# Larger row groups, one-bank column sums with prefix scans, last rows loaded in shrinking pieces, and stores moved to the sync engine, for the diagonal of a 2-D prefix sum

## The chip, the cores and the metric

The kernel runs on one core of a Trainium2 chip. The metric is device time in microseconds (us), the median of several runs. The profile shows one run. Its span, from the first to the last instruction, is 1.6 to 2.2 us shorter than the measured time of these kernels, because it leaves out what lies around the instructions. All times on the time axis below are counted from the start of the span.

Names: PE is the matrix engine, DVE the vector engine, ACT the scalar engine, POOL the GpSimd engine, and SP the sync engine, which computes nothing and here only issues DMAs. In these traces each engine works through its own queue of instructions in order (experiment 8 shows a matmul held up for that reason). A DMA "lands" when the last of the DMA engines that share it, 16 for every load here, has reported its part. PSUM is the memory into which PE adds up its results. A scan is one instruction that writes a running sum along a row.

## The reference

```python
def setup_inputs():
    B, H, W = 4, 4224, 4224
    return {"x": np.random.randn(B, H, W).astype(np.float32)}

def reference(x):
    ps = np.cumsum(np.cumsum(x, axis=1), axis=2)
    diag = np.diagonal(ps, axis1=1, axis2=2)
    return np.cumsum(diag, axis=1).astype(np.float32)
```

The diagonal element `ps[n, n]` is the sum of the square `x[0:n+1, 0:n+1]`. So it grows from n-1 to n by an "L": row n up to the diagonal, and column n above the diagonal. Call that increment `s[n]`. The output is the prefix sum of the prefix sum of `s`. The kernel therefore reads every element once (285 MB), adds the part of each row left of the diagonal along the row (DVE and ACT), adds the part of each column above the diagonal down the column (PE, with a vector of ones), and then does two prefix sums over 4224 numbers per batch.

## The kernel before

It goes through the rows in groups of 256 (two neighbouring rows to a partition), with one group of 128 rows at the end of each batch. POOL loads a group with one DMA that also turns fp32 into bf16. Nine buffers let the loads run far ahead. Row sums go to DVE (`reduce_sum`) and ACT (`activation` with an accumulated sum), column sums to PE, spread over three PSUM tiles.

```python
    groups = [(g * 256, 2) for g in range(16)] + [(4096, 1)]      # shortened
    strips = ctx.enter_context(tc.tile_pool(name="strips", bufs=9))
    ...
        for gi, (row0, pack) in enumerate(groups):
            ...
                strip = strips.tile([P, PACK, N], BF16, name="strip")
                nc.gpsimd.dma_start(out=strip, in_=x[b, row0 : row0 + gw, :].rearrange(...))
            ws = scalar_cols(row0)
            nc.vector.reduce_sum(out=rsv[:, gi, :pack], in_=strip[:, :pack, ws:diag_hi], axis=AX.X)
            for q in range(pack):
                ...                                   # mask the diagonal block, column sums of it on PE
                    nc.scalar.activation(out=dump[:, :ws], in_=strip[:, q, :ws], func=ACT.Copy,
                                         accum_out=sas[:, gi, q : q + 1])
            ...                                       # column sums right of the diagonal on PE
            ...                                       # every 512 columns: copy sums out, scans by single adds
        ...                                           # six fp32 matmuls with triangular weights
        nc.scalar.copy(out=out_sb[nm1 : nm1 + 1, :], in_=out_ps[nm1:NB, :])

        nc.gpsimd.dma_start(
            out=out[b].rearrange("(nb t) -> nb t", t=P), in_=out_sb[:NB, :]
        )
```

POOL issues the loads, and POOL also stores the result.

## Time and profile before

| | |
|---|---|
| time, median of 3 runs | 683.05 us (683.02 to 683.14) |
| span of the profiled run | 681.2 us |
| first load packet | 2.7 us |
| a 256-row group lands every | 9.99 us (4.325 MB read: 433 GB/s) |
| a 128-row group | 5.035 us |
| last load landed | 666.4 us |
| last landing to end of span | 14.8 us |

The rows on packets and landings come from the trace's records of the packets and of the semaphore increments that report them.

First, the page of the kernel before: shares of the span, then the 40 slices of DMA share (9 is 90% or more) and of GB/s written, then the DMA queues with packets, MB and the share of the 16 engines' time.

```profile
PE 181.6 (27%) x1212; PEld 61.6 (9%) x1212; DVE 275.7 (40%) x765; ACT 169.5 (25%) x281; POOL 41.3 (6%) x87
...
DMA  8999999999999999999999999999999999999990
GB/s 179 219 218 210 222 215 213 221 215 214 220 211 221 219 209 222 216 213 221 213 217 220 209 221 220 210 220 217 212 223 214 215 222 210 218 219 213 219 201 3
...
q0 software_dynamic: 9920, 142.81, 98.5%
q8 instruction: 9, 0.15, 0.1%
q14 instruction: 10, 0.08, 0.0%
```

The load queue keeps the DMA engines busy 98.5% of the time and no compute engine is busy for half of it. The GB/s row counts bytes written, which are half of the bytes read, since fp32 becomes bf16: 217 there is 433 read. It is level between the first slice (179) and the last two (201 and 3). The waits say the same. The columns of the next fence are: engine, line, what it waited for, total us, number of waits, longest wait.

```profile
DVE rsv L211 <- DMA strip<-in_x_dram: 337.3, 64, 9.1
...
ACT dump L237 <- DMA strip<-in_x_dram: 290.3, 52, 8.6
...
PE cps L248 <- DMA strip<-in_x_dram: 273.7, 48, 14.2
```

So DVE, ACT and PE wait for data, and work taken from them in the middle of the run gains nothing. What can be gained lies before the first packet, in the rate and the number of bytes and packets, and after the last landing. Here are the two ends of the timeline (start, duration in us, engine, line, operation, and in brackets the idle time before it and what ended it), and the last piece of the chain of work.

```profile
1.31 1.23 POOL L65 DMA_DIRECT2D strip<-in_x_dram  x2 [0.80 <-POOLq L331]
...
14.11 0.69 DVE L211 TENSOR_REDUCE rsv<-strip 128x2 f32<-128x512 bf16 x1 [7.71 <-DMA strip<-in_x_dram]
```

```profile
666.48 2.28 DVE L211 TENSOR_REDUCE rsv<-strip 128x1 f32<-128x2048 bf16 x1
...
673.42 0.26 ACT L312 COPY out_sb<-out_ps 1x128 f32<-1x128 f32 x1 [1.53 <-PE out_ps L309]
673.97 0.53 POOL L314 DMA_DIRECT2D out_dram<-out_sb  x1 [81.42 <-ACT out_sb L312]
```

```profile
673.95 0.55 POOLq L342
```

The last row sum begins at 666.48, when the last group has landed, and the last copy of the result ends at 673.68: 7.2 us of dependent work. Then POOL issues the store. It lands at 675.6, but the span ends at 681.2. The chain's last line names POOL. Behind POOL's last instruction stands a drain, which the page does not count as busy; in the trace it lasts from 673.95 to 680.45, 6.5 us. After it come 0.7 us of a barrier of all engines.

### The profile page before, as it was taken

The page shows a single profiled execution, that of the slowest core. Times are in us where ns is not written, and L with a number is a line of the kernel's source. Part 1 is how long each engine was busy: PE and PEld are TensorE (multiplying, and loading weights), DVE is VectorE, ACT ScalarE, POOL GpSimd, SP SyncE. Part 2 cuts the span into 40 slices and gives each one's busy share as a digit, 9 for nine tenths or more (in the row PEclk, how much of TensorE's full clock was granted, in tenths as well). Part 3 has the DMA queues.
Part 4 walks back from the last instruction along what each step waited for, and adds up shares of the span by engine and source line. Part 5 has one row for each costly group of instructions (what it writes and reads, how often), then busy time and mean ns, then how long its engine had stood idle before and what let it go on. Part 6 is the DMA issues. An engine that isn't in the chain of part 4 may idle for free.

```text
span 681.2 us, 3798 instructions
## 1 busy us (share of the span) xinstructions
PE 181.6 (27%) x1212; PEld 61.6 (9%) x1212; DVE 275.7 (40%) x765; ACT 169.5 (25%) x281; POOL 41.3 (6%) x87
## 2 busy tenths in 40 slices
PE   1243132111442232221233422321124422322112
PEld 0011000000110000000111100000011110000001
DVE  3243245456333333355622342443552323434553
ACT  0001123334101122244400121332440011323442
POOL 2200000000200000000020000000011000000000
PEclk9965555555555555555567555555555555555555
DMA  8999999999999999999999999999999999999990
GB/s 179 219 218 210 222 215 213 221 215 214 220 211 221 219 209 222 216 213 221 213 217 220 209 221 220 210 220 217 212 223 214 215 222 210 218 219 213 219 201 3
DMA packets 9939, 143.04 MB, mean 210 GB/s; under 512 B 1172, under 2 KB 1216, under 8 KB 1216
## 3 DMA queue, kind: packets, MB, share of 16 engines
q0 software_dynamic: 9920, 142.81, 98.5%
q8 instruction: 9, 0.15, 0.1%
q14 instruction: 10, 0.08, 0.0%
HBM read 285.47 MB, written 0.07 MB: 419 GB/s over the span
## 4 chain that ended last, share of the span: by engine, by line
issue 36%; DMA 30%; another core or an unknown queue 21%; DVE 9%; POOL 1%; PE 1%; ACT 1%; POOLq 0%
DMA strip<-in_x_dram 30%; DVE rsv L211 7%; DVE mu L218 1%; POOL strip L203 1%; PE cps L227 1%; ACT c_row L161 1%; DVE cs_col L179 0%; DVE ccs_col L184 0%; PE cps L248 0%; POOL out_dram L314 0%; PE colps L163 0%; DVE aint L261 0%; ACT s_col L283 0%; DVE aint L258 0%
## 5 line engine op out<-in xcount | busy, mean ns | idle before, releaser
L211 DVE TENSOR_REDUCE rsv<-strip 128x2 f32<-128x1536 bf16 (+13 forms) x68 | 178.9, 2630 | 337.3 <-DMA strip<-in_x_dram 337.3
L237 ACT ACTIVATE dump<-strip 128x512 bf16<-128x512 bf16 (+12 forms) x100 | 131.6, 1316 | 291.9 <-DMA strip<-in_x_dram 290.3
L248 PE MATMUL cps<-strip,ones_col 128*1 128x512 bf16 (+2 forms) x640 | 125.7, 530 | 273.7 <-DMA strip<-in_x_dram 273.7
L227 PE MATMUL cps<-mu,ones_col 128*1 128x256 bf16 x132 | 46.8, 372 | 196.0 <-DVE mu L218 196.0
L161 ACT CAST c_row<-cps 1x512 bf16<-1x512 f32 (+1 forms) x36 | 19.4, 540 | 176.0 <-PE cps L248 165.1
L248 PEld LDWEIGHTS <-ones_col 128*1 128x1 bf16 x640 | 27.2, 93 | 304.1 <-issue 300.1
L203 POOL DMA_DIRECT2D strip<-in_x_dram x62 | 32.9, 541 | 297.8 <-DMA strip<-in_x_dram 278.5
L218 DVE SCALAR_TENSOR_TENSOR mu<-strip,um 128x256 bf16<-128x256 bf16 x132 | 49.9, 414 | 0.0
L179 DVE TENSOR_TENSOR cs_col<-cs_col,s_col 128x1 f32<-128x1 f32 x128 | 20.3, 158 | 48.4 <-ACT s_col L283 47.0
L227 PEld LDWEIGHTS <-ones_col 128*1 128x1 bf16 x132 | 13.1, 100 | 229.1 <-issue 228.6
L184 DVE TENSOR_TENSOR ccs_col<-ccs_col,cs_col 128x1 f32<-128x1 f32 x128 | 19.7, 154 | 1.3 <-DVE cs_col L179 0.4
L267 PE MATMUL colps<-aint,sc 128*128 128x1 bf16 x260 | 17.5, 170 | 7.8 <-DVE aint L261 7.8
L314 POOL DMA_DIRECT2D out_dram<-out_sb x4 | 2.1, 534 | 275.2 <-ACT out_sb L312 143.4
L237 ACT ACTIVATION_READ_ACCUMULATOR dump<-strip 128x1 f32 x100 | 18.6, 186 | 0.0
L267 PEld LDWEIGHTS <-sc 128*128 128x128 bf16 x260 | 12.3, 105 | 48.8 <-issue 48.1
L163 PE MATMUL colps<-one_one,c_row 1*128 1x1 bf16 x132 | 9.1, 166 | 12.3 <-ACT c_row L161 11.9
L261 DVE TENSOR_TENSOR aint<-aint,ruv 128x2 bf16<-128x2 bf16 (+1 forms) x68 | 10.9, 160 | 2.1
L218 DVE DVE_READ_ACCUMULATOR mu<-strip,um 128x1 f32 x132 | 10.9, 82 | 0.0
L258 DVE TENSOR_TENSOR aint<-rsv,sas 128x2 bf16<-128x2 f32 (+1 forms) x68 | 10.6, 156 | 0.1
L283 ACT COPY s_col<-colps 128x4 f32<-128x4 f32 (+1 forms) x36 | 5.8, 162 | 14.7 <-PE colps L163 14.7
L147 DVE MEMSET cps<- 128x512 f32 x12 | 5.8, 485 | 4.8 <-ACT c_row L161 4.3
L163 PEld LDWEIGHTS <-c_row 1*128 1x128 bf16 x132 | 6.1, 102 | 14.8 <-ACT c_row L161 14.5
(37 smaller groups left out, 33.9 us busy)
## 6 DMA issues: line engine op xcount, KB each, us to landing
strip<-in_x_dram POOLq DMA_DIRECT2D x64, 2112.0 KB, 74.5
strip<-in_x_dram POOLq DMA_DIRECT2D x4, 1056.0 KB, 74.4
out_dram<-out_sb POOLq DMA_DIRECT2D x4, 16.5 KB, 8.4
```

The source lines that it names most:

```text
L161: nc.scalar.copy(out=c_row[:, lo:hi], in_=chunk_slice(lo, hi))
L163: nc.tensor.matmul(colps[:, k : k + 1], lhsT=c_row[:, k * P : (k + 1) * P], rhs=one_one, start=False, stop=False, skip_group_check=True,)
L179: nc.vector.tensor_add(out=cs_col[:, k + 1 : k + 2], in0=cs_col[:, k : k + 1], in1=s_col[:, k : k + 1],)
L184: nc.vector.tensor_add(out=ccs_col[:, k + 1 : k + 2], in0=ccs_col[:, k : k + 1], in1=cs_col[:, k : k + 1],)
L203: nc.gpsimd.dma_start(out=strip, in_=src)
L211: nc.vector.reduce_sum(out=rsv[:, gi, :pack], in_=strip[:, :pack, ws:diag_hi], axis=AX.X,)
L218: nc.vector.scalar_tensor_tensor(out=mu[:, :gw], in0=strip[:, q, diag_lo:diag_hi], scalar=1.0, in1=upper_masks[pack][q], op0=ALU.mult, op1 ...
L227: nc.tensor.matmul(chunk_slice(diag_lo, diag_hi), lhsT=ones_col, rhs=mu[:, :gw], start=False, stop=False, skip_group_check=True,)
L237: nc.scalar.activation(out=dump[:, :ws], in_=strip[:, q, :ws], func=ACT.Copy, accum_out=sas[:, gi, q : q + 1],)
L248: nc.tensor.matmul(chunk_slice(col, nxt), lhsT=ones_col, rhs=strip[:, q, col:nxt], start=False, stop=False, skip_group_check=True,)
L261: nc.vector.tensor_sub(out=aint[:, gi, :pack], in0=aint[:, gi, :pack], in1=ruv[:, gi, :pack])
L267: nc.tensor.matmul(colps[:, k : k + 1], lhsT=scatters[pack][q][par], rhs=aint[:, gi, q : q + 1], start=False, stop=False, skip_group_check ...
```

## The change

Its intent was to take less time before the first packet and after the last one: groups of 384 rows (three neighbouring rows to a partition, one DMA each); column sums of all groups in one PSUM bank, put into their row of it by a one-hot weight matrix; two scan instructions in place of chains of single adds; the last 384 rows of the last batch loaded in shrinking pieces; the first piece of them (a "head" of 128 rows x 1056 columns) loaded as fp32 by SP at the very start, before POOL's queue gets going; output stores issued by SP. The core of the diff, long parts cut:

```diff
-    PACK = 2
-    GROUP_ROWS = P * PACK
+    F = 3
+    GW = P * F
+    NG = N // GW
-    strips = ctx.enter_context(tc.tile_pool(name="strips", bufs=9))
+    strips = ctx.enter_context(tc.tile_pool(name="strips", bufs=6))
+    HEAD = 1056
+    TB = N - P
+    head = last.tile([P, HEAD], FP32, name="head")
+    nc.sync.dma_start(out=head, in_=x[LB, TB:N, N - HEAD : N])
+    sel = consts.tile([P, 2 * NG - 1], BF16, name="sel")          # zeros, one column of ones
+    def selector(j):
+        return sel[:, NG - 1 - j : 2 * NG - 1 - j]
 ...
+            if j < ng:
+                matmul(d[:, lo:hi], selector(j), rhs, start=first["d"])
 ...
+    def scans(d, rows, width, init1, init2, c12):
+        nc.vector.tensor_tensor_scan(out=c12[:rows, 0, :width], data0=ones_row[:rows, :width],
+            data1=d, initial=init1, op0=ALU.mult, op1=ALU.add)
+        nc.vector.tensor_tensor_scan(...)                         # the same over the first scan
 ...
+        # last batch, rows 3840 to 4095: pieces of columns, the diagonal's first
+        cuts = [r0, 2176, 832, 0]
+        nc.gpsimd.dma_start(out=strip[:, :2, r0:N], in_=src[:, :, r0:N])
+        for c1, c0 in zip(cuts[:-1], cuts[1:]):
+            nc.gpsimd.dma_start(out=strip[:, :2, c0:c1], in_=src[:, :, c0:c1])
+        # the last 128 rows, without the head
+        tcuts = [N - HEAD, 1584, 528, 0]
+        for c1, c0 in zip(tcuts[:-1], tcuts[1:]):
+            nc.gpsimd.dma_start(out=tail[:, 0, c0:c1], in_=x[b, TB:N, c0:c1])
 ...
+        for i, (c1, c0) in enumerate(zip(cuts[:-1], cuts[1:])):
+            ws = (c1 - c0) // 2
+            for q in range(2):
+                act_sum(lsa[:, q, i : i + 1], strip[:, q, c0 : c0 + ws])
+            nc.vector.reduce_sum(out=lrs[:, :, i + 1], in_=strip[:, :2, c0 + ws : c1], axis=AX.X)
+        ...                                                       # lrows = row sums of these 256 rows
+        for q in range(2):
+            matmul(d_last[:, q : gw : 2], lrows[:, q : q + 1], ident)
+        scans(d_last, 1, GW, lcarry[:, 0:1], lcarry[:, 1:2], lc)
+        nc.sync.dma_start(out=out[b, r0 : r0 + gw].unsqueeze(0), in_=lc[:, 1, :gw])
+        ...                                                       # tail: sums tsum, matmuls into fin
+        nc.vector.tensor_add(out=yl, in0=fin, in1=lc[:, 1, gw:GW])
+        nc.sync.dma_start(out=out[b, TB:N].unsqueeze(0), in_=yl)
-        nc.gpsimd.dma_start(
-            out=out[b].rearrange("(nb t) -> nb t", t=P), in_=out_sb[:NB, :]
-        )
```

## The prediction

> **What bounds the kernel now.** The load stream. The page shows the DMA engines 98.5% busy, while DVE is at 40%, PE 27%, ACT 25%; 285.47 MB are read in a 681.2 us span. In the landings of the loads (decoded from the trace), a 256-row strip (4.325 MB read) lands every 9.98 us, 433 GB/s, from start to end, and the 128-row strips take 5.02 us; no gap at the batch borders. The waits agree: DVE, ACT and PE wait mostly for strip DMAs (337, 290, 274 us). So arithmetic in the middle is free.
>
> The span as a sum: first packet at 2.7 us; about 1.4 us of ramp and completion; 64 x 9.98 + 4 x 5.02 = 658.8 us of stream; one DMA engine ends about 3.3 us behind the first (a lag that grows in jumps near instruction-fetch packets); last landing about 666.4. Then (timeline of the end): 7.0 us of arithmetic to the last copy at 673.7; POOL store issued at 674.0, landed about 675.7; POOL's drain, which begins right behind its store, ends only at 680.5, and 0.7 us of barrier follow to 681.2. Tail: 14.7 us.
>
> **What the change does.**
> 1. 384-row groups: longer packets (3 rows instead of 2). From 9.98 against 2 x 5.02 a packet costs some 7.5 ns beyond its bytes, so 43 groups take 642.4 us instead of 643.7. Worth about 1.3 us. The pieces at the end give back about 0.6 us.
> 2. Head (0.54 MB, 1.25 us of stream) on SP at the start: starts perhaps 0.5 us before POOL's loads do. Worth up to 0.5 us.
> 3. Fewer instructions (an estimate from the loops: about 2400 against 3798), so fewer fetches, less lag: 0.5 to 1 us.
> 4. One-hot sums, one bank, scans: hidden chains replace hidden chains. DVE needs about 8.5 us for the widest group (1.04 ns per column), below the 14.9 us it takes to land. Worth 0.
> 5. The tail. The last piece is 528 columns, but DVE runs in order: the strip's reduction (1.0 us), four small sums (0.7), two fp32 matmuls (1.0), two scans (1.2 to 1.9), then the tail's reductions of 792, 1056 and 528 columns (2.9) that queue behind the scans, matmul 0.65, add 0.2. From the last landing that is about 4.5 us instead of 7.0.
> 6. Store on SP: landing about 2 us (estimate; the Trainium skill, "DMA: Bandwidth & Descriptors", section "Anatomy of one DMA", gives about 2.0 us fixed per DMA; the POOL store here took 1.7). The gain is elsewhere: POOL's last instruction becomes a load issued long before, so its 6.5 us drain is hidden, and the end is store + about 0.9 us. Worth nearly 5 us, the largest term.
>
> Tail 4.5 + 2.0 + 0.9 = 7.4 instead of 14.7. Last landing 664.3. Span about 671.7; the measured time is 1.9 us above the span: 673.6 us, 1.4% faster.
>
> **What would show it.** Right: stream at 433 to 435 GB/s; last landing near 664; last landing to end 6.5 to 8.5 us; DVE gapless over the tail reductions behind the scans. Wrong on step 6: POOL's drain still ends last. Wrong on step 1: groups land off 14.94 us.
>
> **What would make it wrong.** Small pieces costing far more per packet; head traffic slowing the first group; scans of 2 us each; or a shorter tail from reordered DVE work plus a larger gain from long packets (then over 2%, below 669.4).
>
> Range 670.3 to 677.0 us. Faster by over 2%: 0.08; within 2%: 0.91; slower: 0.01.

## The result, and the profile after

The kernel after takes 674.39 us (median of 4 runs, 674.34 to 674.50), against 683.03 us for the kernel before in the same rounds. The ratio is 0.9873, with a 95% interval from 0.9859 to 0.9887: 1.3% faster. Here and below a ratio is the mean time of one kernel's fast runs over that of the other's of the same rounds, so it is not quite the ratio of the medians that are quoted.

The page after, the same lines:

```profile
PE 232.5 (35%) x852; PEld 91.2 (14%) x852; DVE 259.3 (39%) x370; ACT 153.9 (23%) x249; POOL 31.8 (5%) x67
...
DMA  9999999999999999999999999999999999999994
GB/s 202 217 215 218 217 217 217 217 217 217 217 219 217 217 218 217 217 217 217 217 217 218 218 217 217 217 215 217 218 217 217 217 217 218 217 217 217 217 201 76
...
q0 software_dynamic: 7712, 142.47, 99.0%
q1 hardware_dynamic: 234, 0.61, 0.3%
q8 instruction: 6, 0.10, 0.1%
q14 instruction: 6, 0.05, 0.0%
```

There are 2608 instructions instead of 3798 and 12 instruction packets instead of 19. SP's queue (q1) appears. The stream is as full and as level as before. DVE's wait is again for the data; PE now waits for DVE's masked block, which waits for the data:

```profile
DVE mu L240 <- DMA strip<-in_x_dram: 380.9, 41, 11.7
PE d L156 <- DVE mu L240: 318.5, 43, 37.2
```

The start and the end of the timeline:

```profile
0.81 0.40 SPq L55 DMA_DIRECT2D head<-in_x_dram  x1
...
1.32 1.19 POOL L60 DMA_DIRECT2D strip<-in_x_dram  x2 [0.80 <-POOLq L384]
...
19.81 1.35 DVE L252 TENSOR_REDUCE rs<-strip 128x3 f32<-128x1152 bf16 x1 [13.92 <-DMA strip<-in_x_dram]
```

SP issues the head at 0.81 and its first packet starts at 1.8; the first packets of POOL's loads follow at 3.5. At the end DVE is the engine to read:

```profile
650.74 6.15 DVE L252 TENSOR_REDUCE rs<-strip 128x3 f32<-128x5760 bf16 x1
...
658.29 1.88 DVE L334 TENSOR_REDUCE lrs<-strip 128x2 f32<-128x1664 bf16 x1
...
663.25 0.98 DVE L334 TENSOR_REDUCE lrs<-strip 128x2 f32<-128x832 bf16 x1
...
665.40 0.96 DVE L362 TENSOR_REDUCE tsum<-strip 128x1 f32<-128x792 bf16 x1
...
666.29 0.14 DVE L343 TENSOR_TENSOR lrows<-l,l 128x2 f32<-128x2 f32 x1
666.36 1.23 DVE L362 TENSOR_REDUCE tsum<-strip 128x1 f32<-128x1056 bf16 x1
...
667.89 1.00 DVE L190 TENSOR_TENSOR_SCAN lc<-ones_row,lcarry,d_last 1x384 f32<-1x384 f32 x1 [0.30 <-PE d_last L156]
668.82 0.67 DVE L362 TENSOR_REDUCE tsum<-strip 128x1 f32<-128x528 bf16 x1
669.42 0.99 DVE L198 TENSOR_TENSOR_SCAN lc<-ones_row,lcarry,lc 1x384 f32<-1x384 f32 x1
...
670.82 0.23 SPq L369 DMA_DIRECT2D out_dram<-yl  x1
```

POOL issues nothing after 634.5, and no POOL line is left at the end. POOL's drain is still there in the trace, from 634.5 to 665.4, 2.1 us after the last landing; it has become invisible because the rest ends later. The last load lands at 663.3. DVE runs on until its last add ends at 670.8, though, with no gap over 0.3 us: the row sums of the last piece of the 256 rows (832 columns, landed at 659.5) start only at 663.25. ACT, in contrast, is done with its last sum at 662.4. The busy time of each engine in 3 us windows (PE, PE weight load, DVE, ACT, POOL, each with its instructions in brackets, then the clock, the DMA share and GB/s):

```profile
661.00:664.00 3.00, 0.92 (x10) 0.34 (x10) 3.00 (x4) 0.95 (x2) 0.00 (x0) 0.50 0.41 71
664.00:667.00 3.00, 0.58 (x3) 0.34 (x4) 3.00 (x11) 0.00 (x0) 0.00 (x0) 0.50 0.03 5
```

The sum of both kernels, from the records of the traces:

| us | predicted change | before | after | measured change |
|---|---|---|---|---|
| last landing | 666.4 to 664.3 | 666.4 | 663.3 | -3.1 |
| last landing to last compute | 7.0 to 4.5 | 7.3 | 7.5 | +0.2 |
| last compute to end of span | 7.5 to 2.9 | 7.5 | 2.0 | -5.5 |
| span | 681.2 to 671.7 | 681.2 | 672.8 | -8.4 |
| time | 673.6 | 683.0 | 674.4 | -8.6 |

So the time is within 0.8 us of the prediction, but the parts are not. The landing came earlier and the store went faster than foretold, and the compute in the tail did not get shorter at all. The experiments take these apart.

### The profile page after: what moved, and what is told of

Same layout as the page of the kernel before. It is cut to its first block, busy times and chain, and to the rows that moved or that the text cites. A ratio compares the mean times of both kernels' runs of the same rounds, so it can differ in the third digit from the quotient of the medians.

```text
span 672.8 us, 2608 instructions
## 1 busy us (share of the span) xinstructions
PE 232.5 (35%) x852; PEld 91.2 (14%) x852; DVE 259.3 (39%) x370; ACT 153.9 (23%) x249; POOL 31.8 (5%) x67
## 4 chain that ended last, share of the span: by engine, by line
another core or an unknown queue 51%; DVE 36%; DMA 11%; issue 1%; POOL 0%; PE 0%; DVEq 0%; POOLq 0%
DVE rs L252 24%; DMA strip<-in_x_dram 11%; DVE mu L240 9%; DVE lrs L334 1%; DVE c L198 1%; DVE c L190 1%; DVE y L281 0%; DVE y L273 0%; DVE tsum L362 0%; POOL strip L60 0%; DVE lc L190 0%; DVE lc L198 0%; PE d_last L156 0%; DVEq L240 0%
## 5 line engine op out<-in xcount | busy, mean ns | idle before, releaser
L165 ACT ACTIVATE dump<-strip 128x192 bf16<-128x192 bf16 (+11 forms) x124 | 141.1, 1138 | 507.7 <-DMA strip<-in_x_dram 505.1
L240 DVE SCALAR_TENSOR_TENSOR mu<-strip,um 128x384 bf16<-128x384 bf16 x129 | 65.5, 554 | 380.9 <-DMA strip<-in_x_dram 380.9
L252 DVE TENSOR_REDUCE rs<-strip 128x3 f32<-128x1152 bf16 (+10 forms) x43 | 169.8, 3950 | 27.5 <-DMA strip<-in_x_dram 27.5
L156 PE MATMUL d<-mu,sel 128*11 128x384 bf16 x129 | 59.2, 476 | 318.8 <-DVE mu L240 318.5
L156 PE MATMUL d<-strip,sel 128*11 128x384 bf16 x630 | 161.9, 431 | 0.0
L156 PEld LDWEIGHTS <-sel 128*11 128x11 bf16 (+1 forms) x794 | 86.7, 109 | 538.8 <-issue 515.2
L60 POOL DMA_DIRECT2D strip<-in_x_dram x43 | 23.0, 535 | 507.5 <-PE d L156 256.7
L156 PE MATMUL d_last<-strip,sel 128*1 128x384 bf16 (+1 forms) x32 | 14.2, 477 | 84.8 <-DMA strip<-in_x_dram 84.8
L165 ACT ACTIVATION_READ_ACCUMULATOR dump<-strip 128x1 f32 x124 | 23.1, 186 | 0.0
L156 PE MATMUL d<-ident,rows 128*11 128x128 f32 (+1 forms) x24 | 5.8, 415 | 19.9 <-DVE sa L219 13.2
L308 POOL DMA_DIRECT2D strip<-in_x_dram x3 | 1.6, 538 | 43.1 <-DMA strip<-in_x_dram 28.5
L304 POOL DMA_DIRECT2D strip<-in_x_dram x3 | 2.1, 708 | 6.7 <-DMA strip<-in_x_dram 6.7
```

The source lines that it names most:

```text
L60: nc.gpsimd.dma_start(out=t, in_=x[b, r0 : r0 + GW, :].rearrange("(p f) w -> p f w", f=F),)
L156: nc.tensor.matmul(o, lhsT=lhsT, rhs=rhs, start=start, stop=False, skip_group_check=True)
L165: nc.scalar.activation(out=dump[:, :w], in_=src, func=ACT.Copy, accum_out=acc)
L240: nc.vector.scalar_tensor_tensor(out=mu, in0=strip[:, q, lo:hi], scalar=1.0, in1=um3[q], op0=ALU.mult, op1=ALU.mult, accum_out=ru[:, g, q ...
L252: nc.vector.reduce_sum(out=rs[:, g, :], in_=strip[:, :, ws:hi], axis=AX.X)
L304: nc.gpsimd.dma_start(out=strip[:, :2, c0:c1], in_=src[:, :, c0:c1])
```

## The experiments

All twelve kernels ran with timed rounds beside the kernel before, whose median was between 683.04 and 683.24 us each time. "Tail" below means the time from the last landing of a load to the end of the span in the profiled run: 14.8 us before and 9.5 us after. The theory at the outset: POOL's drain behind a store is worth about 5 us; the rest comes from the stream. The rivals: the store's engine does not matter, and the gain comes from the arithmetic and the pieces.

### 1. Before, with its stores on SP

```diff
-        nc.gpsimd.dma_start(
+        nc.sync.dma_start(
             out=out[b].rearrange("(nb t) -> nb t", t=P), in_=out_sb[:NB, :]
         )
```

> The kernel before with only its four output stores moved from POOL to SP. Theory (the hidden drain of POOL): POOL's last instruction becomes a load, its drain ends about 2 us after the last landing (as in the kernel after, 665.4 against 663.4) and the span ends about 2 us after the store is issued at 674: span near 676 instead of 681.2, time about 678, some 5 us faster. Rival (the gain of the change is in the arithmetic and the pieces, a store is a store): within 1 us of 683.

Measured: correct, 678.35 us (678.24 to 678.44), ratio 0.9931. The last landing is where it was (666.3), the last copy ends at 673.6, and the tail is 9.8 instead of 14.8 us. The end of the timeline:

```profile
673.38 0.26 ACT L312 COPY out_sb<-out_ps 1x128 f32<-1x128 f32 x1 [1.53 <-PE out_ps L309]
673.66 0.29 SPq L314 DMA_DIRECT2D out_dram<-out_sb  x1
```

The theory holds: the one word `sync` in place of `gpsimd` gives 4.7 of the 8.6 us that the whole change gains, with no arithmetic touched. Most of this is the drain, but not all: the store itself also lands earlier, at 675.0 instead of 675.6. POOL's drain ends at 669.2 here, 2.8 us after the last landing, where about 2 had been expected.

### 2. After, with its last store on POOL

```diff
-        nc.sync.dma_start(out=out[b, TB:N].unsqueeze(0), in_=yl)
+        nc.gpsimd.dma_start(out=out[b, TB:N].unsqueeze(0), in_=yl)
```

> The kernel after with only its last store (128 values) moved from SP to POOL. Theory: the store is issued near 670.9, lands about 1.7 us later, POOL's drain ends about 6.5 us after the issue and the span about 0.7 us after that: span near 678, time 679 to 680, some 5 us slower than after. Rival: the drain is long only where loads were issued shortly before it, and here they were issued 36 us earlier: at most 1 us slower than after.

Measured: correct, 678.97 us, but the runs scatter: 678.25, 678.95, 678.99, 679.39. The tail is 13.3 us, 3.8 more than after. The chain of waits ends on POOL again:

```profile
671.74 0.53 POOLq L395
```

The mechanism is confirmed from the other side: one store of 128 values on POOL costs 3.8 us or more. Its size was off: the drain lasts 4.8 us here (671.7 to 676.5), where 6.5 had been read from before. So it is not a fixed time, neither from its start nor from the landing (3.2 us after this store's landing, 4.8 after the one of before; where no store follows, 2.1 us after the last load in the kernel after, 2.8 in kernel 1 and 1.9 in kernel 6). What sets it stays open. The other part of the +4.6 us is that the loads landed 0.7 us later in the profiled run; see experiments 7 and 12.

### 3. After, with packets of one row

```diff
-            in_=x[b, r0 : r0 + GW, :].rearrange("(p f) w -> p f w", f=F),
+            in_=x[b, r0 : r0 + GW, :].rearrange("(f p) w -> p f w", f=F),
```

The same DMAs and bytes, but a partition takes three rows that do not lie together, so a packet is one row. The result is wrong.

> The kernel after, but a partition of a group takes rows p, p+128 and p+256 instead of three neighbours: same bytes, same DMAs, three packets of one row each in place of one of three rows (the result is wrong on purpose). Theory (about 10 ns per packet beyond its bytes, from 5.035 us for 8 one-row packets per engine, 9.99 for two rows and 14.966 for three): a group takes 15.105 us, 43 groups 6 us more, time about 680. Rival (packet length is worth nothing and the shorter stream came from less lag alone): within 0.5 us of after.

Measured: 678.95 us (678.94, 678.96, 678.97 and one run at 677.57). A group's landing, taken on the engine that is first, goes from 14.966 to 15.018 us: 0.052 us for 16 more packets on each engine, 3.3 ns a packet. Over the 42 intervals that is 2.2 us. The other 2.2 us of the later last landing in the profiled run are 0.7 us in the first group and 1.5 us more lag of the last engine behind the first, which one of the four runs did not have. So both sides missed. Packet length does matter, but the price per packet is a third of the 10 ns that had been fitted; the 128-row group's 5.035 us, on which that fit stood, may hold a cost for each DMA beside that for each packet, or be scatter (its four landings took 5.005 to 5.069 us). That is not tested. Worked out from the two landing rates, the 384-row groups are worth about 0.9 us: 129 blocks of 128 rows at 4.989 us instead of 4.996 (659.5 us for all 132 blocks before).

### 4. After, with the head on POOL

```diff
-    nc.sync.dma_start(out=head, in_=x[LB, TB:N, N - HEAD : N])
+    nc.gpsimd.dma_start(out=head, in_=x[LB, TB:N, N - HEAD : N])
```

> The kernel after with the fp32 head loaded by POOL, first in its queue, instead of by SP. Theory (the head fills the time before POOL's first packets): the first packet moves from 1.9 to about 2.7 us and everything behind it by 0.8 us or a little more; time about 675.2. Rival (the head costs its 1.25 us wherever it is issued): no change.

Measured: correct, 675.27 us (675.26 to 675.44), 0.9 us more than after. The first packet of all starts at 2.7 instead of 1.8 us, and the last landing is at 664.1 instead of 663.3; the tail is 9.5, as after. So the head on SP is worth 0.9 us here: its packets start 0.9 us before the first packet of any kernel in which POOL issues all loads (before, 4 and 12: 2.7). The prediction had allowed up to 0.5.

### 5. After, with more of the 256 rows on ACT

```diff
-            ws = (c1 - c0) // 2
+            ws = (c1 - c0) * 3 // 4
```

> The kernel after, with three quarters of each of the 256-row pieces summed by ACT instead of half. Theory (the tail is DVE's queue: it is busy without a gap from the last full group's landing at 649.2 to 667.7 and ACT idles after 662.4): DVE is freed of 1920 columns, 2.0 us at 1.04 ns each, and the end comes some 2 us earlier: time 672 to 673. Rival (the end hangs on the last pieces' landing and the chain of dependent sums and scans behind it): within 0.3 us of after, or slower by ACT's added 1.6 us.

Measured: correct, 674.70 us (673.80, 674.68, 674.73, 674.99), no faster than after. The tail in the profiled run is 8.7 instead of 9.5 us. The theory that the tail is simply the sum of DVE's work fell: 2.0 us were taken from DVE and at most 0.8 came back. DVE now waits for 1.5 us ahead of the first of the last two scans, on a matmul of the sums `lrows`, which the compiler had queued on DVE behind the sums of the tail pieces:

```profile
666.14 0.14 DVE L343 TENSOR_TENSOR lrows<-l,l 128x2 f32<-128x2 f32 x1
667.75 1.00 DVE L190 TENSOR_TENSOR_SCAN lc<-ones_row,lcarry,d_last 1x384 f32<-1x384 f32 x1 [1.47 <-PE d_last L156]
```

### 6. After, with the last rows in two loads instead of seven

```diff
-        nc.gpsimd.dma_start(out=strip[:, :2, r0:N], in_=src[:, :, r0:N])
-        for c1, c0 in zip(cuts[:-1], cuts[1:]):
-            nc.gpsimd.dma_start(out=strip[:, :2, c0:c1], in_=src[:, :, c0:c1])
+        nc.gpsimd.dma_start(out=strip[:, :2, :], in_=src)
 ...
-        for c1, c0 in zip(tcuts[:-1], tcuts[1:]):
-            nc.gpsimd.dma_start(out=tail[:, 0, c0:c1], in_=x[b, TB:N, c0:c1])
+        nc.gpsimd.dma_start(out=tail[:, 0, : N - HEAD], in_=x[b, TB:N, : N - HEAD])
```

> The kernel after, with the 256 rows loaded by one DMA and the tail's 3168 columns by one more, the sums left cut as they are. Last landing some 0.3 us earlier (fewer packets and DMAs). Theory (DVE's queue is the tail): DVE idles from 656.8 until the 256 rows land at about 659.2, and the end moves by that, 2 to 2.5 us later: time 676 to 677. Rival (the pieces are what makes the tail short): the last sums start only at the last landing, as before the change, 4 us or more later.

Measured: correct, 676.89 us (676.73 to 677.10), 2.5 us more than after. The last landing is 0.4 us earlier (662.9), which is what the seven pieces cost the stream; DVE idles for 2.4 us, from 656.8 to 659.2, and the tail grows to 12.3 us. The theory's numbers held:

```profile
659.21 0.43 DVE L313 SCALAR_TENSOR_TENSOR mu<-strip,um 128x256 bf16<-128x256 bf16 x1 [2.41 <-DMA strip<-in_x_dram]
```

The shrinking pieces thus gain by keeping DVE fed from 657 on; that the very last piece is small gains nothing here, since DVE reaches it 5.5 us after it landed.

### 7. After, with 1188 idle instructions more

```diff
+            if whole:
+                for _ in range(36):
+                    nc.scalar.copy(out=idle[0:1, 0:1], in_=step[0:1, 0:1])
```

> The kernel after, with 36 one-element copies added to ACT in each group of the first three batches: 1188 more instructions, as many as before had, none on the critical path (ACT stays below 13 us in the 14.97 us of a group). Theory (instruction fetches hold up single DMA engines and make the lag of the last one): 18 or 19 fetch packets instead of 12, a spread of the last landing near 2.5 to 3 us instead of 1.7, time 0.8 to 1.3 us more, about 675.4. Rival (the lag has another source): within 0.3 us of after.

Measured: correct, 676.32 us (676.17 to 676.47), 1.9 us more than after, with nothing on the critical path. The DMA queues:

```profile
q8 instruction: 6, 0.10, 0.1%
q14 instruction: 16, 0.12, 0.0%
```

With the larger program there are 22 instruction packets by the page. The lag of the last DMA engine behind the first grew by 3.3 us from the first group to the last (0.4 to 3.7); after it had grown by 0.9 us with 12 packets, and before by 2.8 us with 19. The tail stayed at 9.5 us. The first engine to report the last load did so at 661.6 in both kernels, so only some engines are late. When the lag rises also points to the fetches: in before, after and kernel 7 it rises by more than 0.15 us from one landing to the next 18 times (6, 3 and 9), and in each of these intervals an instruction packet started, though only a quarter to a third of all intervals hold one. So fetching instructions delays single DMA engines, the delay is kept to the end, since the load queue leaves them no idle time in which to catch up (99.0% busy), and the last landing is that of the worst engine. That a smaller program lands earlier is shown. Its size was underestimated: the lag at the end is 3.3 us before and 1.7 after, so it is worth 1.6 us rather than the 0.5 to 1 of the prediction.

### 8. After, with a cheaper group loaded last of the full ones

```diff
-        for g in range(ng):
+        for g in range(ng) if whole else [0, 1, 2, 3, 5, 6, 7, 8, 9, 4]:
```

> The kernel after, with the last batch's full groups loaded in the order 0, 1, 2, 3, 5, 6, 7, 8, 9, 4. Group 4 needs 1056 columns of DVE sum per row where group 9 needs 1920, so DVE is done with the last full group 2.7 us earlier. Theory (DVE's queue, filled by that group, delays the pieces' sums): the end comes 2 to 2.7 us earlier, time 671.7 to 672.5. Rival (the chain behind the last landing): no change.

Measured: correct, 673.88 us (673.66, 673.69, 674.07, 674.65), half a microsecond faster than after. The tail is 8.6 instead of 9.5 us: again no more than a third of the 2.7 us that DVE was spared. Where the rest went can be read off. DVE is through with the last of the 256 rows' sums at 661.6, 2.7 us earlier than after, and then waits 1.7 us for `carry_ps`:

```profile
660.59 0.98 DVE L334 TENSOR_REDUCE lrs<-strip 128x2 f32<-128x832 bf16 x1
663.31 0.15 DVE L271 COPY carry<-carry_ps 10x2 f32<-10x2 f32 x1 [1.74 <-PE carry_ps L156]
```

On PE, and in the same run:

```profile
662.51 0.59 PE L156 MATMUL fin<-wtri,tsum 128*1 128x128 f32 x2 [5.42 <-ACT dump L165]
663.03 0.20 PE L156 MATMUL carry_ps<-c,earlier 10*10 10x2 f32 x2
```

The matmul of `carry_ps` needs only DVE's scan, which ended at 660.7. It stands in PE's queue behind a matmul that waits for an ACT sum of a tail piece. So the new theory, which 9 to 11 test, is: in the tail it counts what a dependent step stands behind in the in-order queues; taking work from DVE turns into waits unless the queues are rearranged as well.

### 9. Group order, tail pieces on ACT, and queues held in program order

From kernel 8, the end of the program was rewritten so that the chain `lrows`, `d_last`, scan, scan comes first and the tail pieces' sums (now on ACT alone) and matmuls come behind it; each DVE, ACT and PE instruction there was tied behind the one before it on its engine, so that the compiler keeps this order. The arithmetic is the same.

```diff
+        keep = (lambda i: i) if whole else tc.keep_in_program_order
 ...
+        for q in range(2):
+            keep(matmul(d_last[:, q : gw : 2], lrows[:, q : q + 1], ident))
+        keep(nc.vector.tensor_copy(out=lcarry, in_=lcarry_ps))
+        finish()                                      # the first ten groups' result, while PE works
+        keep(nc.vector.tensor_tensor_scan(...))       # twice
 ...
+        for k, (c1, c0) in enumerate(zip(tcuts[:-1], tcuts[1:])):
+            keep(act_sum(tsum[:, k : k + 1], tail[:, 0, c0:c1]))
+            keep(matmul(fin, tsum[:, k : k + 1], wtri))
```

> The kernel after with group 4 loaded last of the full groups (as in e8_group_order), the three tail pieces summed by ACT alone (2.9 us off DVE), and the queues of DVE, ACT and PE at the end held in program order, so that lrows, d_last and the two last scans no longer stand behind the tail pieces' sums and matmuls. Theory (e5 and e8 gained under 1 us because a full in-order queue was replaced by waits: what counts is where the serial chain lrows, d_last matmul, scan, scan, add stands in the queues): DVE is through with the 256 rows at 661.5, lrows 662, d_last 663.1, scans 665.1, the ACT sum of the last piece 665.0 and its matmul 665.7, last add ends near 666, span 668 to 668.5, time about 670, 4.4 us faster than after. Rival (the chain behind the last landing is as long as it shows, whatever the order): no better than e8_group_order, 673.7.

Measured: correct, 670.38 us (669.65, 669.78, 670.98, 671.08), ratio 0.9813 to before. The tail is 4.7 us, half of after's 9.5. In this profiled run the last load landed at 664.6, 1.3 us later than after (its lag, see 12), so the clock times below probably stand 1.3 us later than in its faster runs, which were not profiled:

```profile
662.16 0.98 DVE L350 TENSOR_REDUCE lrs<-strip 128x2 f32<-128x832 bf16 x1
...
663.64 0.16 DVE L366 TENSOR_TENSOR lrows<-l,l 128x2 f32<-128x2 f32 x1
...
664.93 1.00 DVE L372 TENSOR_TENSOR_SCAN lc<-ones_row,lcarry,d_last 1x384 f32<-1x384 f32 x1
...
665.97 1.00 DVE L376 TENSOR_TENSOR_SCAN lc<-ones_row,lcarry,lc 1x384 f32<-1x384 f32 x1
...
666.41 0.58 PE L156 MATMUL fin<-wtri,tsum 128*1 128x128 f32 x2 [0.18 <-ACT dump L165]
...
667.08 0.28 DVE L389 TENSOR_TENSOR yl<-fin,lc 1x128 f32<-1x128 f32 x1
```

The last scan and the last tail matmul now end within 0.1 us of each other, at 667.0, 2.4 us after the last landing. 4.4 us had been expected, and 4.7 us of tail, or 4.0 us of median time, were gained. The rival (673.7) is out. But three things changed at once here (group order, tail sums on ACT, held queues), so this run does not show that the order of the queues did it; 10 and 11 take it apart, and give the held order a smaller share than the theory did.

### 10. The same without the group order

```diff
-        order = list(range(ng)) if whole else [0, 1, 2, 3, 5, 6, 7, 8, 9, 4]
+        order = list(range(ng)) if whole else list(range(ng))
```

> As e9_order, but with the groups loaded in their old order (group 9 last). DVE comes out of group 9's sum at 656.8, ends the 256 rows' sums near 664 and the scans near 667.6: last add ends near 667.9, span near 670, time 671.5 to 672, 2.5 to 3 us faster than after. If the group order is worth nothing once the queues are in order, it equals e9_order.

Measured: correct, 672.55 us (672.22, 672.46, 672.64, 674.23), tail 7.5 us. That is 2.0 us less tail than after, somewhat less than expected. The group order, which gained 0.9 us of tail by itself (8), gains 2.7 us on top of kernel 10, which has the held queues and the tail sums on ACT.

### 11. Only the tail pieces' sums moved to ACT

```diff
-            if i == 0:
-                ws = (c1 - c0) // 2
-                act_sum(...)                          # half of the first piece
-            ...
-            nc.vector.reduce_sum(out=tsum[:, k : k + 1], in_=tail[:, 0, c0:c1], axis=AX.X)
+            act_sum(tsum[:, k : k + 1], tail[:, 0, c0:c1])
             matmul(fin, tsum[:, k : k + 1], wtri)
```

> The kernel after with only the tail pieces' sums moved to ACT (2.9 us off DVE), queues left as the compiler orders them; there the matmuls of the tail sums stand before d_last on PE. Theory of order: d_last waits for ACT's last sum and its matmul (about 666), scans end near 669, gain under 1.2 us: time 673.2 to 674.4. Rival (only the sum of DVE's work counts): 2.9 us faster than after, 671.5.

Measured: correct, 672.74 us (672.71 to 672.77), 1.65 us faster than after, tail 7.8 us: between the two expectations, so neither was right as stated. The order had been expected to stop PE's matmul of `lrows` at a tail sum; in fact it started at 665.6 as soon as DVE had `lrows` ready, which still stood behind other work:

```profile
665.64 0.51 PEld L156 LDWEIGHTS d_last<-ident,lrows 128*1 128x1 f32 x4 [0.50 <-DVE lrows L343]
```

Against kernel 10 (7.5 us) the held order alone is worth just 0.3 us. The 2.7 us of the group order in kernel 9 over kernel 10, and the 0.9 us of it in kernel 8, show that the parts do not add up: what the group order is worth depends on what else stands in the chain. One combination was not run: the group order with the tail sums on ACT, and the queues as the compiler orders them. So how much of the 2.7 us needs the held order is not shown.

### 12. Kernel 9 with the head on POOL

> e9_order with the head loaded by POOL, as in e4_head_pool. The runs of e9_order fall at 669.7 and at 671.0, and in its profile one engine starts its first group packet 0.7 us after the others and takes 3.1 us for it: a lag of 2.5 us on the first landing, kept to the end. Theory (the lag comes where the head on SP's queue and the first group on POOL's meet on one engine, by chance): all six runs within 0.4 us of each other, first group's spread near 0.8 us, time near 670.6 (669.7 plus the 0.9 us that e4 lost). Rival (the lag has nothing to do with the head's queue): two clusters 1.3 us apart again, near 670.6 and 671.9.

The edit is that of experiment 4. Measured: correct, 670.65 us (670.59 to 670.79, 5 runs), ratio 0.9816, tail 4.7 us, spread of the first group's landing 0.5 us. The theory's prediction held to the tenth. In kernels 9 and 10, which load the head by SP, the profiled run had a first spread of 2.5 and 2.3 us, with one packet that started late (at 5.0 and 5.3 us) and took long (3.1 and 2.8 us instead of 1.9). All 9 runs with the head on POOL (experiments 4 and 12) lie within 0.2 us of their kernel's median; of the kernels with the head on SP, some scatter by 1 to 2 us (2, 3, 5, 8, 9, 10) and some do not (after, 6, 7, 11). So the head on SP brings 0.9 us and, in some programs and runs, costs 1.3 us again. Why one program is hit and another is not stays open.

Kernels 9 and 12 beat both kernels: 1.9% and 1.8% faster than before, and 0.6% faster than after by the medians (which were not measured in the same rounds).

## Why the prediction was right

The prediction said 673.6 us, between 670.3 and 677.0, and within 2% of before. The measured time is 674.39 us. Point by point:

| step of the prediction | predicted, us | measured, us | by |
|---|---|---|---|
| what bounds the kernel: the load stream, at 433 to 435 GB/s | no change | 433.0 before, 433.5 after | landing rates |
| 1. longer packets, larger groups | -1.3 | -0.9 | landing rates, experiment 3 |
| 1. pieces at the end | +0.6 | +0.4 | experiment 6 |
| 2. head on SP | up to -0.5 | -0.9 | experiment 4 |
| 3. smaller program, less lag | -0.5 to -1 | -1.6 | experiment 7 and the spreads |
| 4. one bank, one-hot sums, scans | 0 | not tested alone; the stream shows no loss | landing rates, waits |
| 5. compute after the last landing | 7.0 to 4.5 | 7.3 to 7.5 | timelines |
| 6. store and end | 7.5 to 2.9 | 7.5 to 2.0 | experiments 1 and 2 |

The mechanism that carries most of the gain was right: POOL's drain behind a late store was on the end of the chain, and a store issued by SP takes it away (4.7 us by experiment 1, and 3.8 us or more back by experiment 2). The store itself was mis-sized. "Landing about 2 us" took 1.1 us from the issue at 670.82 to SP's passing its wait at 671.91. The Trainium skill, "DMA: Bandwidth & Descriptors", section "Anatomy of one DMA", gives about 2.0 us as the fixed cost of a DMA issued by GpSimd; the prediction used it for a store issued by SP, which took about half. POOL's store of before took 1.7 us.

The step that failed is the fifth: "From the last landing that is about 4.5 us instead of 7.0." The sum began at the landing of the last piece of the 256 rows, as if DVE were free by then. DVE's price per column was read correctly: 1.04 ns (4.42 us for 4096 columns and 0.69 for 512, before), in line with the Trainium skill, "VectorE: DVE Perf Modes", section "The perf-mode tier table", which gives `tensor_reduce` no faster mode than one element per cycle for any type. But DVE had 7.6 us of work from the last full group alone, which landed at 649.2, and 2.9 us more for the first ten groups' scans and result. The row sums of that last piece began 3.8 us after it had landed. From their start to the end of the last add it took 7.5 us, and the pieces that the prediction lists add up to about 7.7 to 8.4: the length was close, the start was not. The order was wrong too, for the prediction had written the scan chain before the tail sums, while the compiler's order put tail sums between its steps; that cost less, for the held order alone was worth 0.3 us (experiment 10 against 11). The prediction's own mark, 6.5 to 8.5 us from the last landing to the end, was missed: it was 9.5. This term is off by 2.7 us (2.5 us less foretold, 0.2 us more measured). The others made up for 1.9 us of it: 0.8 lag, 0.4 head, 0.9 store and end and 0.2 pieces, less 0.4 groups. That leaves the 0.8 us between prediction and result. That the total came so close is luck: errors of up to 2.7 us with opposite signs.

And the term that was mis-sized is a real reserve: experiment 9 took 4.7 us out of the tail by moving and reordering the same sums.

## What to carry to other kernels

When a kernel is bound by its load stream, look at what stands before the first packet and behind the last landing, and there at every engine's end, the one that issues DMAs included: an engine whose last act is a store may go on for microseconds after it (POOL here, for 6.5 and 4.8 us), and moving that one store to another engine can be the largest gain of a long change (4.7 of 8.6 us). In such a tail, count each engine's backlog at the moment the last data land, not just the work of the last data, and read the order in the queues that the compiler made; work moved off a full engine pays in full only if the dependent chain does not then wait behind something else (of the tail, at most 0.8 of 2.0 us came back in experiment 5, 0.9 of 2.7 in 8, 1.7 of 2.9 in 11). A smaller program can be faster even where its instructions are idle, because instruction fetches hold up the same DMA engines (1.9 us for 1188 idle instructions, experiment 7).

## What the Trainium skill lacked or had wrong

- "VectorE: DVE Perf Modes", section "The DRAIN you can't avoid", says of the drains that the runtime adds in the pre- and postamble that they are about 12 ns on all five engines. It has nothing on the drain that ends the kernel's own program (L342 before, L395 after). POOL's took 6.5 us behind a store (before), 4.8 us (experiment 2), and waited out the outstanding loads where POOL had issued nothing after them (30.9 us in the kernel after, until 2.1 us after the last landing; 1.9 to 2.8 us after it in kernels 6 and 1).
- "DMA: Bandwidth & Descriptors", section "Issuing engines are not separate DMA queues", says that starting DMAs on several engines at once only saves the sequencer's time for the issue. It leaves out what the choice of engine costs at the end of a program: the issue took 0.5 us, and moving the stores from POOL to SP gained 4.7 us (experiment 1).
- The page on instruction fetches ("Runtime: NRT & Kernel Launch", section "Instruction fetch mechanics") has no figure for what they cost a load stream that fills the DMA engines: the lag of the slowest DMA engine grew by 0.9 us over a run with 12 instruction packets and by 3.3 us with 22 (experiment 7; 1.9 us of time).
- The fixed 2.0 us of "DMA: Bandwidth & Descriptors", section "Anatomy of one DMA", is given for GpSimd, and the section has no such sum for SP. A store of 512 bytes from SP took 1.1 us from issue to the end of the wait for it.
- The table of "VectorE: DVE Perf Modes", section "The perf-mode tier table", has no row for the scan; that it runs at half throughput stands elsewhere in the skill, on the page with the DVE opcode table, but without a time. Here 384 elements took 0.93 us on 10 partitions and 1.00 us on one, 2.4 to 2.6 ns per element, over twice the reduction's 1.08 (4.42 us for 4096).
